# 22 of the 38 early expert tiles of a PEER layer in two float32r parts instead of whole float32 rows

## The chip, the cores and the metric

The kernel runs on one core of one Trainium2 chip. The metric is the time of one execution on the device in microseconds (us); of several runs the median is given. A profiled execution has a span, from its first to its last instruction, and a time of its own that is a little longer than the span.

The engines are named as in the profile: PE is TensorE (matmuls), PEld its weight loads, DVE is VectorE, ACT is ScalarE, POOL is GpSimd, SP is SyncE, which issues most of the DMAs.

## What is computed

An encoder block: a mixer (RWKV-7 and pooling), then an expert layer, then a last norm. The change is in the expert layer. Its reference, cut to what matters:

```python
def peer_ffn(h, wq, keys, u_tab, v_tab):
    def block_fn(xb):                       # 128 tokens at a time, 4 blocks
        q = (xb @ wq).reshape(T, PEER_HEADS, 2, PEER_KHALF)
        s = jnp.einsum('thpc,hpnc->thpn', q, keys)
        v1, i1 = lax.top_k(s[:, :, 0], 16)
        v2, i2 = lax.top_k(s[:, :, 1], 16)
        ...
        idx = jnp.take_along_axis(cidx, pos, axis=-1)
        gate = jax.nn.softmax(sc, axis=-1)
        ug = jnp.take(u_tab, idx, axis=0)
        act = jax.nn.gelu(jnp.einsum('td,thkd->thk', xb, ug))
        vg = jnp.take(v_tab, idx, axis=0)
        return jnp.einsum('thk,thkd->td', gate * act, vg)
```

There are 512 tokens, 1024 model dimensions, 16384 experts and 8 heads of 16 picks.

## The kernel before

The expert layer (`peer`, from line 948) treats three of the four token blocks, 384 tokens, densely and the fourth by gathering. For the dense blocks the 16384 experts are 128 tiles of 128. An **up tile** is the product of one tile of `u` with the 384 tokens, over 8 slices of the 1024 dimensions, followed by a Gelu on ACT into a tile `gl`. A **down step** multiplies `gl` by the gates `gt` of that tile of experts, and multiplies the result by the tile of `v` into six PSUM banks `o`.

Up tiles exist in two forms. `up_parts` (L990) takes a tile in two float32r parts: `split` (L978) casts the raw tile `ur` to `uh` on ACT (L980) and subtracts on DVE to get the low part `ul` (L982); then there are three matmuls for each of 8 slices, `uh` with `hh` (L994), `uh` with `hl` (L995) and `ul` with `hh` (L996), 24 in all. The generator `ups` (L1013) takes **early** tiles, which are computed before the down side starts, with whole float32 rows: one matmul for each slice, `ur` with `hx` (L1020), 8 in all. The profile shows each of these float32 matmuls as two records, so 16 a tile. There are 38 early tiles (608 records): ten whose `gl` is stored in DRAM for later, and 28 that stay in SBUF. The other 90 tiles go through `up` (L1003) inside the loop over down steps.

While `ups` runs, the rest of the selection runs beside it. For each token block DVE makes the top-16 picks (`top16`, `topk`: L1412 to L1471), and `transposed` (L1485) turns a dense block's picks and gates with three PE transposes (`sc<-ident`, L1491), a copy on ACT to `pk` (L1494) and a remainder on DVE (L1496). Then `encode` (L1172) makes for each 8 tokens a **code block** of three tiles on DVE, `a2` (L1187), `b1` (L1189) and `bh` (L1191); `b1` is then scaled by a remainder on DVE or POOL (L1194) or with eight small instructions on ACT (L1197). At most three code blocks are held (`NB = 3`). `gates` (L1201) multiplies a code block on PE in two halves of 8 matmuls (`pg`, L1212 and L1213), ACT copies each half to `sg` (L1215), and every second block SP writes `sg` to the DRAM tensor `gdram` (L1218). The down side reads it back as `gt`.

The order of all this is written as a string of letters, `PROG2`, one letter for one step of a generator (`u` is a step of `ups`, two slices of a tile; `e` and `p` are steps of `encode` and `gates`). A scheduler then places the instructions of each engine; on each engine they run in the placed order. PSUM has two buffers for `d` (up tiles) and two for `pg`; SBUF has three for `ur`, two for `uh` and two for `ul`.

Of the kernel before, what the change touches and what calls it, by code (L numbers as in the profile page):

```python
# [10 lines left out]
F32 = mybir.dt.float32  # L11
# [4 lines left out]
AF = mybir.ActivationFunctionType  # L16
# [7 lines left out]
DT = D // 128  # L24
# [38 lines left out]
SX = "VVVV"  # L63
SH = "VGVGVGVG"
NHF = 3
NST = 2
PORD = [6, 2, 7, 10, 3, 17, 19, 14, 11, 18]
PROG = 'mmmmsmmmmss2ms22sss2sms2msms2sssmssmm2smssmsmsmsmss2sms3smsmssmss2vvmp3msmmj32mj33mjm33jmggmm33mmjjmmv2m33SvSSSSvSSmSwSmSpSpSSgCSaaSSaaSSDalhSSSlfffffafhaSafSSaSfSaSSfaSSahaSSffflffhSahfaafafaaJJaafffJfhlfaaJafJaJabbfnbbfbbflnbbfbfbfbnfbbbbfbnbbbbnfbnnfbnoxoobxoxxoxoboxoooxboobxyyoooooyyXyXXXyXyXXXXyYYYYYYYYY'
# [79 lines left out]
def mixer(ctx, rs, tc, t, x_dram, x2_dram, ident, vec, vecs, dbg, load_vectors):  # L148
# [51 lines left out]
    with ExitStack() as s1:  # L200
        ld = s1.enter_context(tc.tile_pool(name="ld", bufs=1, side="right"))
        st = s1.enter_context(tc.tile_pool(name="st", bufs=NST, side="right"))
        x = [ld.tile([128, D], F32, name=f"x{i}") for i in range(NT)]
# [8 lines left out]
        for i in range(NT):  # L212
# [5 lines left out]
            for q in range(2):  # L218
                pt = bank([128, 4, 128])
                for d in range(4):  # L220
                    PE.transpose(pt[:, d], x[i][:, (4 * q + d) * 128:(4 * q + d + 1) * 128], ident)
                hf = st.tile([128, 4, 128], F32, name="hf", bufs=NHF)
                V.tensor_tensor(hf, pt, vecs("n1")[:, 4 * q:4 * q + 4, None].to_broadcast([128, 4, 128]), op=ALU.mult)
# [724 lines left out]
def peer(ctx, rs, tc, t, X2, x2_dram, ident, out, dbg):  # L948
    nc = tc.nc
    V, A, G, PE, SY = nc.vector, nc.scalar, nc.gpsimd, nc.tensor, nc.sync  # L950
    pool = lambda n, b, **k: ctx.enter_context(tc.tile_pool(name=n, bufs=b, **k))
    GT, DTS = 3, [1, 2, 0]
    ND = 128 * len(DTS)
# [5 lines left out]
    ps_d = pool("psd", 2, space=PSUM)  # L959
# [16 lines left out]
    E = {"V": V, "G": G}  # L976

    def split(src, n, pool, eng=V):  # L978
        hi = pool.tile([128, D], F32R, name=n + "h")
        A.copy(hi, src)  # L980
        lo = pool.tile([128, D], F32R, name=n + "l")
        eng.tensor_tensor(lo, src, hi, op=ALU.subtract)  # L982
        return hi, lo

    def up_load(e):
        raw = ub.tile([128, D], F32, name="ur", bufs=3)
        SY.dma_start(raw, t["uT"][e])
        return raw

    def up_parts(uh, ul):  # L990
        ps = ps_d.tile([128, ND], F32, name="d")
        for d in range(DT):
            c = slice(d * 128, d * 128 + 128)
            PE.matmul(ps, uh[:, c], hh[:, d, 0:ND], start=d == 0, stop=False)  # L994
            PE.matmul(ps, uh[:, c], hl[:, d, 0:ND], start=False, stop=False)  # L995
            PE.matmul(ps, ul[:, c], hh[:, d, 0:ND], start=False, stop=d == DT - 1)  # L996
            if d in (1, 3, 5):
                yield
        g = glp.tile([128, ND], F32, name="gl")
        A.activation(g, ps, AF.Gelu)  # L1000
        yield g
# [9 lines left out]
    early = later + list(range(AHEAD))  # L1011

    def ups():  # L1013

        raw = {e: up_load(e) for e in early[:3]}
        for k, e in enumerate(early):
            ur = raw.pop(e)
            ps = ps_d.tile([128, ND], F32, name="d")
            for d in range(DT):
                PE.matmul(ps, ur[:, d * 128:d * 128 + 128], hx[:, d], start=d == 0, stop=d == DT - 1)  # L1020
                if d in (1, 3, 5):
                    yield
            if k + 3 < len(early):
                raw[early[k + 3]] = up_load(early[k + 3])
            g = glp.tile([128, ND], F32, name="gl")
            A.activation(g, ps, AF.Gelu)  # L1026
            if e in later:
                SY.dma_start(gld[later.index(e)], g)
            else:
                Gl[e] = g  # L1030
            yield

    with ExitStack() as pa:
# [9 lines left out]
        hx = pa.enter_context(tc.tile_pool(name="hx", bufs=1)).tile([128, DT, ND], F32, name="hx")  # L1043
# [196 lines left out]
        def chained(gens):  # L1240
# [3 lines left out]
        ub = glp = None  # L1244
        order = ORDER
        streams = {z: stream(z, g, *needs) for z, g, *needs in (
            ("n", normed()), ("O", opened(), "n"), ("q", queries(), "n"), ("k", scores(), "n"), ("t", tops()),
            ("r", chained([choose(n, 0) for n in order])), ("R", chained([select(n) for n in order])),
            ("c", swap(), "kt"), ("e", encode(), "c"), ("p", gates(), "c"), ("u", ups(), "O"))}
        left = {"n": 12, "O": 1, "k": 16, "t": 64, "c": 1}  # L1250
        engines = [{"PE": PE, "V": V, "A": A, "G": G, "SY": SY}[z].engine for z in ORD.split(",")]
# [39 lines left out]
    with ExitStack() as pb:  # L1291
# [51 lines left out]
        for e in range(NE):  # L1343
            n = e + AHEAD
# [6 lines left out]
            raw = vb.tile([128, D], F32, name="vr")  # L1351
# [9 lines left out]
            for k in range(share(e), share(e + 1)):  # L1361
                u = vb.tile([128, D], F32, name="gat", bufs=6)
# [180 lines left out]
```

## Time and profile before

| | us |
|---|---|
| time, median of 3 runs | 1752.48 (1751.49 to 1756.0) |
| the profiled execution: its own time | 1755.74 |
| the profiled execution: its span | 1754.0 |
| PE busy in the span | 1633.1 (93%) |
| DVE busy | 1287.5 (73%) |
| ACT busy | 642.7 (37%) |
| POOL busy | 518.1 (30%) |
| up tiles with whole rows, L1020 | 215.8 busy, 608 records |
| up tiles in two parts, L994, L995, L996 | 242.3, 242.0, 242.2 busy, 720 records each |

Shares over the whole span hide that the stages differ. The early tiles run from 565.5 to 836.8 us of the span, the tiles in two parts from 836.8 us. A matmul's record reaches from its start to its modelled end, and records of neighbours overlap; the pace of a row of matmuls is therefore read from start to start.

### The profile page before, as it was taken

Reading aid. Unit: us, or ns where it says so; the run is one execution under the profiler, and the core shown is the slowest. Engines: PE = TensorE matmul, PEld = TensorE weight load, DVE = VectorE, ACT = ScalarE, POOL = GpSimd, SP = SyncE. Lnnn points to the kernel's source line nnn. Section 1 sums busy time; section 2 is a strip of 40 time slices with the busy share of each in tenths; the row PEclk is TensorE's granted clock in tenths of the full one; section 3 lists DMA queues with packets and bytes.
Section 4 is the critical chain, followed back from the end, with each engine's and each line's share of the span. In section 5 each row is a group of like instructions: output and inputs, shape, how many; then the busy total and the mean of one; then the engine's idle time right before and its main releaser. Section 6 shows DMA issues by size and latency. Waiting matters only on the chain.

```text
span 1754.0 us, 25849 instructions
## 1 busy us (share of the span) xinstructions
PE 1633.1 (93%) x9513; PEld 1317.4 (75%) x9513; DVE 1287.5 (73%) x2730; ACT 642.7 (37%) x1090; POOL 518.1 (30%) x355
## 2 busy tenths in 40 slices
PE   6888776899799799999999999999999999999997
PEld 5766664564587456566889999898989989898886
DVE  5665976446589999853467787777777887787776
ACT  4343331121433267353433333333333333333334
POOL 2331432000113000000104454444554554554430
PEclk8788887999899899999999999999999999999999
DMA  3354478760321365454989889989989998887774
GB/s 139 104 139 115 135 156 272 199 213 26 140 85 65 104 229 214 151 201 180 326 270 324 304 325 341 323 312 327 339 305 337 332 314 329 314 321 254 259 261 160
DMA packets 220191, 405.29 MB, mean 231 GB/s; under 512 B 38352, under 2 KB 137168, under 8 KB 216992
## 3 DMA queue, kind: packets, MB, share of 16 engines
q1 hardware_dynamic: 179680, 258.06, 45.1%
q0 software_dynamic: 39808, 144.52, 22.7%
q8 instruction: 75, 1.23, 0.3%
q10 hardware_dynamic: 576, 1.05, 0.2%
q14 instruction: 52, 0.43, 0.1%
HBM read 350.23 MB, written 53.35 MB: 230 GB/s over the span
## 4 chain that ended last, share of the span: by engine, by line
PE 73%; DVE 17%; DMA 5%; ACT 2%; issue 2%; SPq 1%; POOL 0%; DVEq 0%; ACTq 0%; POOLq 0%
PE o L1385 29%; PE d L996 7%; PE d L995 7%; PE d L994 7%; PE d L1020 6%; PE mm L815 2%; DMA UV<-vd 2%; PE a L500 2%; PE mm L323 2%; PE mm L321 1%; PE mm L322 1%; DMA gt<-gdram 1%; DVE pr L1467 1%; PE mm L1095 1%; DVE a L1187 1%
## 5 line engine op out<-in xcount | busy, mean ns | idle before, releaser
L1302 POOL DMA_INDIRECT gat<-in_peer_u,num x128 | 190.5, 1489 | 293.8 <-DVE gat L1308 243.5
L1302 POOL DMA_INDIRECT gat<-in_peer_v,num x128 | 198.4, 1550 | 214.0 <-DVE acc L1310 190.0
L996 PE MATMUL d<-hh,ul 128*128 128x384 f32 x720 | 242.3, 337 | 0.0
L994 PE MATMUL d<-hh,uh 128*128 128x384 f32 x720 | 242.2, 336 | 0.0
L995 PE MATMUL d<-hl,uh 128*128 128x384 f32 x720 | 242.0, 336 | 0.0
L1385 PE MATMUL o<-vl,wh 128*128 128x512 f32 x768 | 238.6, 392 | 2.3 <-DVE vl L982 2.3
L1385 PE MATMUL o<-vh,wh 128*128 128x512 f32 x768 | 238.4, 392 | 0.8 <-ACT wh L1369 0.8
L1385 PE MATMUL o<-vh,wl 128*128 128x512 f32 x768 | 238.3, 391 | 0.0
L1020 PE MATMUL d<-hx,ur 128*128 128x384 f32 x608 | 215.8, 499 | 8.0 <-ACT gl L1026 8.0
L980 ACT CAST uh<-ur 128x1024 fp32r<-128x1024 f32 x90 | 94.8, 1053 | 241.8 <-PE d L995 232.2
L1369 ACT CAST wh<-gl 128x384 fp32r<-128x384 f32 x128 | 65.7, 514 | 303.9 <-PE o L1385 296.0
L1371 DVE TENSOR_TENSOR wl<-gl,wh 128x384 fp32r<-128x384 f32 x128 | 71.3, 557 | 141.0 <-ACT wh L1369 140.2
L1385 PEld LDWEIGHTS o<-vl,wh 128*128 128x128 f32 x768 | 144.3, 188 | 34.9 <-DVE vl L982 3.4
L1385 PEld LDWEIGHTS o<-vh,wl 128*128 128x128 f32 x768 | 144.6, 188 | 31.2
L1020 PEld LDWEIGHTS d<-hx,ur 128*128 128x128 f32 x608 | 111.7, 193 | 72.0 <-ACT gl L1026 8.6
L1310 DVE SCALAR_TENSOR_TENSOR acc<-gat,wg,acc 128x1024 f32<-128x1024 f32 x128 | 163.8, 1280 | 0.9
L982 DVE TENSOR_TENSOR vl<-vr,vh 128x1024 fp32r<-128x1024 f32 x128 | 156.1, 1220 | 9.3 <-ACT vh L980 8.6
L1385 PEld LDWEIGHTS o<-vh,wh 128*128 128x128 f32 x768 | 143.4, 188 | 25.1 <-ACT wh L1369 1.1
L1308 DVE SCALAR_TENSOR_TENSOR gat<-gat,h2g 128x1024 f32<-128x1024 f32 x128 | 153.5, 1218 | 0.0
L980 ACT CAST vh<-vr 128x1024 fp32r<-128x1024 f32 x128 | 135.1, 1055 | 24.5 <-DMA vr<-in_peer_v 22.6
L982 DVE TENSOR_TENSOR ul<-ur,uh 128x1024 fp32r<-128x1024 f32 x90 | 109.9, 1222 | 44.1 <-ACT uh L980 44.0
L995 PEld LDWEIGHTS d<-hl,uh 128*128 128x128 f32 x720 | 135.3, 188 | 4.2
(364 smaller groups left out, 2741.8 us busy)
## 6 DMA issues: line engine op xcount, KB each, us to landing
ur<-in_uT SPq DMA_DIRECT2D x128, 512.0 KB, 5.3
vr<-in_peer_v SPq DMA_DIRECT2D x128, 512.0 KB, 4.1
gdram<-sg SPq DMA_DIRECT2D x24, 1024.0 KB, 3.9
gt<-gdram SPq DMA_DIRECT2D x16, 1536.0 KB, 14.3
wqk<-in_wqk SPq DMA_DIRECT2D x16, 576.0 KB, 3.5
gad<-gs SPq DMA_DIRECT2D x16, 512.0 KB, 3.3
GA<-gad SPq DMA_DIRECT2D x16, 512.0 KB, 4.8
w<-in_w_in SPq DMA_DIRECT2D x15, 512.0 KB, 6.7
```

Of the source, the lines that this page charges most:

```text
L980: A.copy(hi, src)
L982: eng.tensor_tensor(lo, src, hi, op=ALU.subtract)
L994: PE.matmul(ps, uh[:, c], hh[:, d, 0:ND], start=d == 0, stop=False)
L995: PE.matmul(ps, uh[:, c], hl[:, d, 0:ND], start=False, stop=False)
L996: PE.matmul(ps, ul[:, c], hh[:, d, 0:ND], start=False, stop=d == DT - 1)
L1020: PE.matmul(ps, ur[:, d * 128:d * 128 + 128], hx[:, d], start=d == 0, stop=d == DT - 1)
L1302: G.indirect_dma_start(out=u, out_offset=None, in_=t["peer_u" if k < NP else "peer_v"], in_offset=bass.IndirectOffsetOnAxis(ap=num[:, kk:k ...
L1308: V.scalar_tensor_tensor(u, u, 1.0, h2g, op0=ALU.mult, op1=ALU.mult, accum_out=dot[:, kk:kk + 1])
L1310: V.scalar_tensor_tensor(acc, u, wg[:, kk:kk + 1], acc, op0=ALU.mult, op1=ALU.add)
L1369: A.copy(wh, w)
L1371: wi = V.tensor_tensor(wl, w, wh, op=ALU.subtract)
L1385: PE.matmul(O[j][q], a[:, c], b[:, q * 512:(q + 1) * 512], start=e == 0 and n == 0, stop=e == NE - 1 and n == 2)
```

## The change

The first 16 early tiles (`UF = 16`) keep the whole float32 rows. The other 22 go through `split` and `up_parts`, as the 90 later tiles do, with the low part made on the engine that a string `UE` names for each tile, which is DVE (`V`) for all. The split of a tile is written after the second slice of the tile before it. The strings `PROG2` and `BLE` and the buffers are unchanged.

```diff
+UF = 16
+UE = 'VVVV...'
...
         raw = {e: up_load(e) for e in early[:3]}
+        parts = {}
         for k, e in enumerate(early):
-            ur = raw.pop(e)
-            ps = ps_d.tile([128, ND], F32, name="d")
-            for d in range(DT):
-                PE.matmul(ps, ur[:, d * 128:d * 128 + 128], hx[:, d], start=d == 0, stop=d == DT - 1)
-                if d in (1, 3, 5):
-                    yield
+            ur = raw.pop(e) if k < UF else None
+            if ur is not None:
+                ps = ps_d.tile([128, ND], F32, name="d")
+                for d in range(DT):
+                    PE.matmul(ps, ur[:, d * 128:d * 128 + 128], hx[:, d], start=d == 0, stop=d == DT - 1)
+                    if d == 1 and k + 1 >= UF and k + 1 < len(early):
+                        parts[k + 1] = split(raw.pop(early[k + 1]), "u", ub, E[UE[k + 1]])
+                    if d in (1, 3, 5):
+                        yield
+                g = glp.tile([128, ND], F32, name="gl")
+                A.activation(g, ps, AF.Gelu)
+            else:
+                for n, g in enumerate(up_parts(*parts.pop(k))):
+                    if n == 0 and k + 1 < len(early):
+                        parts[k + 1] = split(raw.pop(early[k + 1]), "u", ub, E[UE[k + 1]])
+                    if n < 3:
+                        yield
             if k + 3 < len(early):
                 raw[early[k + 3]] = up_load(early[k + 3])
-            g = glp.tile([128, ND], F32, name="gl")
-            A.activation(g, ps, AF.Gelu)
```

After the change the lines of `peer` from L978 on stand two lines lower and those behind `ups` thirteen lower.

Three places of the new order follow. In names such as `a_6424` the number tells code blocks apart.

**DVE, around the third low part.** Before, these rows run in the last third of the second dense block's encoding; `e_3768` collects the third dense block's picks.

```order
L1470 TENSOR_TENSOR pr<-pr 128x2x64
L1187 TENSOR_TENSOR a_6433<-ior,pk_5828 128x1024
L1189 TENSOR_TENSOR b_6435<-ior,pk_5828 128x1024
L1471 TENSOR_REDUCE e_3768<-pr 128x2x16
L1191 TENSOR_TENSOR bh<-b_6435,pk_5828 128x1024
```

Now, at the place where the third dense block's picks are collected:

```order
L1480 TENSOR_TENSOR pr<-oh,f_6603 128x512 x2
L1200 TENSOR_TENSOR a_6540<-ior,pk_5828 128x1024
L1202 TENSOR_TENSOR b_6542<-ior,pk_5828 128x1024
L984 TENSOR_TENSOR ul<-ur,uh 128x1024
L1204 TENSOR_TENSOR bh<-b_6542,pk_5828 128x1024
L1482 TENSOR_TENSOR pr<-pr 128x2x128
L984 TENSOR_TENSOR ul<-ur,uh 128x1024
L1207 TENSOR_TENSOR b_6542<-b_6542,pk_5828 128x1024
```

The third and the fourth low part stand between the rows of one code block; they are two of nine that stand ahead of the remainder `pk` of the third dense block (L1509, L1496 of before).

**ACT, before the third cast.** Before, the Gelu of an early tile follows the exponential of `gate`:

```order
L1197 ACTIVATE b_6390<-b_6390,lo_5896 128x128 x6
L1477 ACT_TABLE_LOAD
L1477 ACTIVATE gate<-gate 128x128
L1215 ACTIVATE sg<-pg 128x128x4 x2
L1026 ACT_TABLE_LOAD
L1026 ACTIVATE gl<-d 128x384
L1215 ACTIVATE sg<-pg 128x128x4 x2
```

Now the casts stand among them:

```order
L1210 ACTIVATE b_6426<-b_6426,lo_5896 128x128 x6
L1490 ACT_TABLE_LOAD
L1490 ACTIVATE gate<-gate 128x128
L1228 ACTIVATE sg<-pg 128x128x4 x2
L1002 ACT_TABLE_LOAD
L1002 ACTIVATE gl<-d 128x384
L982 CAST uh<-ur 128x1024
L1228 ACTIVATE sg<-pg 128x128x4 x2
L982 CAST uh<-ur 128x1024
```

The third and fourth cast of an early tile stand behind the same two table loads.

**PE, at the transposes of the third dense block.** Before:

```order
L1213 MATMUL pg<-b_6608,a_6606 128x128
L1020 MATMUL d<-hx,ur 128x384 x21
L1491 MATMUL sc<-ident,e_3768 128x128 x2
L1491 MATMUL sc<-ident,gate 128x128
L1020 MATMUL d<-hx,ur 128x384 x12
L1212 LDWEIGHTS a_6741
```

Now (the first three rows end a run of 66 matmuls, where one of 21 stood):

```order
L996 MATMUL d<-hh,uh 128x384
L997 MATMUL d<-hl,uh 128x384
L998 MATMUL d<-hh,ul 128x384
L1504 MATMUL sc<-ident,e_3768 128x128 x2
L1504 MATMUL sc<-ident,gate 128x128
L996 MATMUL d<-hh,uh 128x384
```

The code blocks and transposes keep their places among the slices of the early tiles; each slice of a tile is now three matmuls.

## Rows read from the trace of the kernel before

**Rows 1.** The page: busy tenths of PE and DVE, granted clock, in 40 slices.

```profile
PE   6888776899799799999999999999999999999997
DVE  5665976446589999853467787777777887787776
PEclk8788887999899899999999999999999999999999
```

**Rows 2.** Busy time in three stretches: length, then PE, PEld, DVE, ACT, POOL (instructions), granted clock, DMA.

```profile
691.95:731.40 39.45, 36.23 (x216) 23.68 (x214) 39.42 (x188) 19.05 (x40) 0.00 (x0) 0.98 0.47 166
731.40:836.80 105.40, 105.40 (x535) 66.47 (x534) 45.50 (x85) 46.32 (x110) 1.89 (x1) 0.99 0.54 190
900.00:1700.00 800.00, 799.64 (x3977) 718.20 (x3977) 617.89 (x774) 285.62 (x387) 377.90 (x248) 1.00 0.88 310
```

**Rows 3.** The chain that ended last, 729 to 747 us: start, length, what.

```profile
729.52 0.20 DVE gateg L1476
729.75 0.31 ACT gateg L1477
730.06 0.49 ACT sg L1215
...
731.60 14.54 PE d L1020 x42
746.14 0.33 PE sc L1491 x3
```

**Rows 4.** Timeline of PE, whole-row tiles and code blocks: start, length, what [idle before].

```profile
691.95 0.22 PE L1212 MATMUL pg<-bh,a 128*128 128x128 f16 x1
...
692.87 0.86 PE L1020 MATMUL d<-hx,ur 128*128 128x384 f32 x2
...
715.64 9.24 PE L1020 MATMUL d<-hx,ur 128*128 128x384 f32 x28
724.72 0.22 PE L1212 MATMUL pg<-bh,a 128*128 128x128 f16 x1
...
730.59 0.26 PE L1212 MATMUL pg<-bh,a 128*128 128x128 f16 x1 [2.80 <-ACT sg L1215]
...
731.40 14.74 PE L1020 MATMUL d<-hx,ur 128*128 128x384 f32 x42
745.98 0.38 PE L1491 MATMUL sc<-ident,e 128*128 128x128 f32 x2
```

**Rows 5.** Timeline of PE, tiles in two parts, 54 matmuls of which three stand here.

```profile
836.80 0.63 PE L994 MATMUL d<-hh,uh 128*128 128x384 f32 x1
...
837.45 0.33 PE L996 MATMUL d<-hh,ul 128*128 128x384 f32 x1
...
846.30 0.34 PE L996 MATMUL d<-hh,ul 128*128 128x384 f32 x1
```

**Rows 6.** The page, groups of the split: count, busy us, mean ns, idle before.

```profile
L980 ACT CAST uh<-ur 128x1024 fp32r<-128x1024 f32 x90 | 94.8, 1053 | 241.8 <-PE d L995 232.2
L982 DVE TENSOR_TENSOR ul<-ur,uh 128x1024 fp32r<-128x1024 f32 x90 | 109.9, 1222 | 44.1 <-ACT uh L980 44.0
```

**Rows 7.** Timeline of DVE, 686 to 854 us.

```profile
686.58 0.67 DVE L1187 TENSOR_TENSOR a<-ior,pk 128x1024 f16<-128x1024 f16 x1
...
689.39 0.68 DVE L1187 TENSOR_TENSOR a<-ior,pk 128x1024 f16<-128x1024 f16 x1
690.00 0.69 DVE L1189 TENSOR_TENSOR b<-ior,pk 128x1024 f16<-128x1024 f16 x1
...
738.31 0.28 DVE L1482 TENSOR_TENSOR gateg<-gateg,gs 128x128 f32<-128x128 f32 x1
747.02 0.29 DVE L1496 TENSOR_TENSOR pk<-sc,pk 128x128 f16<-128x128 f32 x1 [8.43 <-ACT pk L1494]
...
852.38 1.22 DVE L982 TENSOR_TENSOR ul<-ur,uh 128x1024 fp32r<-128x1024 f32 x1
853.52 1.22 DVE L982 TENSOR_TENSOR vl<-vr,vh 128x1024 fp32r<-128x1024 f32 x1
```

**Rows 8.** Timeline of ACT: a table load, and eight scalings of one code block.

```profile
702.77 1.28 ACT L1477 ACT_TABLE_LOAD   x1
...
749.89 2.48 ACT L1197 ACTIVATE b<-b,lo 128x128 f16<-128x128 f16 x8 [0.30 <-DVE bh L1191]
```

More of the change, by code (lines that the diff above doesn't have):

```diff
@@ L65 @@
 NHF = 3
+UF = 16
+UE = 'VVVVVVVVVVVVVVVVVVVVVVVVVVVVVVVVVVVVVVVVVVVVVVVVVVVVVVVVVVVVVVVVVVVVVVVVVVVVVVVV'
 NST = 2
```

## The prediction

> **What bounds the kernel now.** I read the 40 slices first [rows 1]: from the twenty-second on PE is at 9 and DVE at 7 or 8, so the down side is PE's; ahead of it the two lines change places, DVE at 9 where PE is at 7 and then PE at 9 where DVE is at 6 and 5. The change lies in that change of places, so I cut the stretch of the 22 tiles out with a table of windows [rows 2]. From 691.95 to 731.40 us DVE is busy for 39.42 of 39.45 us; from 731.40 to 836.80 us PE is busy for all of 105.40 us and DVE for 45.50. The chain that ended last agrees [rows 3]: it runs along DVE up to `gateg` at 729.52, crosses ACT (an exponential and a copy of `sg`) and then stays on PE, 14.54 us of whole-row matmuls first. So a saving on PE counts at its full size after 731 us, and what is added to DVE before that may count too. From 900 to 1700 us PE is busy 799.64 of 800 us, with the same instructions after the change: whatever is won before the down side is kept.
>
> **What an early tile costs on PE.** From 715.64 to 724.72 us 28 records of whole-row matmuls start, one in 0.3243 us [rows 4]; a tile has 16, so 5.19 us. In two parts, 51 matmuls lie between the starts at 837.45 and 846.30 us, 0.1735 us each [rows 5]; a tile has 24, so 4.16 us. The difference is 1.03 us a tile and 22.6 us for 22. Both paces are of the full clock and of the same shapes that the change uses (384 tokens, 128 by 128 weights).
>
> The Trainium skill ("FP8 and Floating Point Precision", section "TensorE Precision Notes") says that true FP32 takes four passes through the array. Three passes for four would save a quarter of 5.19 us, an estimate of 1.30 us a tile and 28.5 us in all. The trace shows less, since a part takes 0.1735 us where a quarter of a whole row takes 0.162; I go by the trace.
>
> **The sum over the stretch.** PE has from 691.95 to 836.80 us, 144.85 us, 360 records of whole rows (22.5 tiles, 116.7 us), 24 code blocks at 0.92 us (one runs from 691.95 to 692.87 [rows 4], 22.1 us) and 0.33 us of transposes [rows 3]: 139.2 us. The other 5.7 us are losses: one wait of 2.80 us for `sg` at 730.59 [rows 4], after which the 42 records take 14.58 us where the pace gives 13.62, at a granted clock that the table puts at 0.98 and 0.99 over the stretches; the rest is small. After the change four whole-row matmuls are left (2.6 us) and 528 matmuls of parts come in (91.6 us): 116.6 us of work, 22.6 us less. What decides is how the 5.7 us of losses change.
>
> **What is added elsewhere.** ACT gets 22 casts of 1.053 us (23.2 us), DVE 22 subtractions of 1.222 us [rows 6], which follow each other at 1.14 us [rows 7]: 25.1 us. DVE has 60 us free in the second stretch [rows 2] and nothing in the first, so place matters. I add the paces of DVE's rows in the new order, from the first row that it shares with the old one (the `a` step at 686.58). Code passes go at 0.6 us [rows 7], the selection rows at what they take in the trace; the same addition over the old order lands on `gateg` within 0.2 us of 738.31 [rows 7].
>
> *To the third low part:* 20 code passes (12.0 us), three low parts (3.4) and the selection rows between them (7.8) are 23.2 us, so it is ready at 709.8 us. PE comes there with 73 code-block matmuls (4.2 us), four whole rows (2.6) and 50 of parts (8.7) after 691.95, at about 707.6. It waits for 2 us. The third cast doesn't make it later: behind the two table loads (1.28 us each [rows 8]) it ends at about 707.3.
>
> *To the third dense block:* 26 code passes, nine low parts (10.3 us) and 26.8 us of selection put `pk` at 739.3 us. PE has its transposes done at 733.5 plus the 2 us, so at 735.5 to 736. Before, it was DVE that waited for PE here, 8.43 us [rows 7]. From `pk` on the first code block takes 2.7 us on DVE and 2.48 us of scalings on ACT [rows 8], to 744.5. PE covers this with the 36 matmuls that stand between (6.2 us), to 742.3: a wait of 2.2 us.
>
> *The rest:* from there PE has 68.8 us of work. DVE has 58 us, with the last 13 low parts. ACT had 46.32 us in 105.40 [rows 2] and gets 13 casts (13.7): 60 us. Neither is full, but both run in order and are at five sixths of PE's time. No row shows waits of this kind; from below they cost nothing, from above one pair of cast and subtraction uncovered at each third tile (13/3 x 2.27 = 10 us). I take 3 us, near the lower end, since the splits are written a tile ahead and before the change PE had no idle time in this stretch [rows 2].
>
> So the stretch ends at 744.5 + 68.8 + 3 = 816.3 us instead of 836.8: 20.5 us earlier. The long wait at 730.59 goes, because the exponential of `gateg` moves behind the third block's first codes; waits of 2.0, 2.2 and 3 us come. The DMAs stay as many: a `ur` tile is loaded once in either form, and its buffer comes free earlier, when the low part is made. SP's queue carries the same loads and writes, and what starts the down side (54 matmuls, then `gt` from DRAM) has the same distance from the last code block. The profiled execution took 1755.74 us, 3.3 above the median; 20.5 us less is 1735.2 beside it and 1732 beside the median.
>
> **Rivals.** *The new waits hide.* If the low parts are ready in time and the 5.7 us go as well, the gain is 22.6 + 5.7 = 28 us: 1724. Against it stands that DVE is full to 731 us [rows 2] and nine low parts are put there.
>
> *DVE stays the bound.* Its chain up to `pk` gets nine low parts and is not shortened by PE's gain. Should the code blocks behind them come late as well, the 10.3 us are lost once and the gain is 12 us: 1740. The Trainium skill ("TensorE: Matmul & The Clock Gate", "Architectural detail: the array is 16x 32x32, not 1x 128x128") says that ACT and DVE take their queues strictly in order. The trace agrees in the 2.80 us that PE waited for a copy standing behind an exponential.
>
> *The queues interlock, and the kernel is slower.* A low part waits for its cast, the cast for scalings and table loads ahead of it, and the codes behind the low part wait with it; PE stands. Its place is the second stretch, where codes and splits alternate. Uncovered, a tile costs a cast and a subtraction, 2.27 us [rows 6]; 22 tiles cost 50 us, and less the 22.6 the result is 27 us slower: 1780. It decides from the point where more than 1.03 us is lost for each tile. For it speaks that two `uh` and two `ul` leave one tile of lead; against it that DVE and ACT have a sixth of the stretch free.
>
> *It evens out.* The same mechanism at half that price takes the 22.6 us: 1750 to 1755. In all of them the clock could add: the one wait of 2.80 us had a loss of about 1 us behind it.
>
> **How the numbers follow.** The forecast, 1727 to 1738, has 0.62; hidden waits (1722 to 1727) 0.10; DVE as bound (1738 to 1747) 0.16; evened out 0.06; slower 0.06. The range from 1724 to 1744 leaves out the last two, the upper end of the third and the lower end of the second, some 2 in 10. A measurement of this kernel can tell about 0.3%, 5.3 us, from no change: faster 0.88, within 0.06, slower 0.06.
>
> **What would show it.** In the profile after, the whole-row records fall to 256, the parts rise to 112 tiles (896 of each line) at a pace of 0.1735 us; the last matmul ahead of the first down step, at 846.30 before, comes about 20 us earlier; PE's long idle time ahead of a `d` matmul is for `ul` near 710 us and for `ACT b` near 743 us, 2 us each, and no wait of 2.8 us for `sg` is left. DVE is full until about 739 us and above 80% from there to the down side. It is wrong if the pace of the parts beside the selection is not 0.1735, if PE's waits in the stretch sum to over 12 us, or if the down side starts earlier but ends no earlier, for instance because `gt` or `vr` land late.

## The result and the profile after

The change takes 1734.28 us (median of 4 runs, 1731.09 to 1735.49), the kernel before 1754.24 us (median of 4, 1751.49 to 1760.95). The ratio is 0.9878, 95% interval 0.9845 to 0.991: 20 us less by the medians and 21 by the ratio, which is one of means, where 20.5 were forecast (1732, range 1724 to 1744). The profiled execution has an own time of 1731.09 us and a span of 1729.4, against 1755.74 and 1754.0.

Of the 24.6 us between the two spans, 3.3 are not the change's: the first matmul of the early tiles starts at 562.44 us where it stood at 565.7, with the same instructions ahead of it. From there to the first matmul of the down side the stretch is 261.6 us (562.44 to 824.03) instead of 281.8 (565.7 to 847.46), 20.2 us shorter; the rest, about 1 us, is the down side. The length of this stretch, called **the stretch** below, is the measure of all the experiments. It has one weakness: every kernel is scheduled anew, and matmuls of later tiles can move across its end. Before the change 54 matmuls in two parts stand between the last early tile and the first matmul of the down side, after it 57, so 0.5 us of the stretch after is work brought forward. Each stretch comes from one profiled execution; the change's own, taken twice, is 261.6 and 262.1.

The 40 slices of the page after, as [rows 1]:

```profile
PE   6888876899899799999999999999999999999997
DVE  5665986437589999995667777777778878787776
PEclk8788887999899899999999999999999999999999
```

From the fifteenth to the eighteenth slice (605 to 778 us) PE and DVE are both at 9. Before, DVE left that level two slices earlier and fell to 3 and 4; it now falls to 5 and 6 only. The windows after, as [rows 2] (length, then PE, PEld, DVE, ACT, POOL, granted clock, DMA), with one more over the whole stretch, first from the trace of before and then from that of after:

```profile
565.00:847.00 282.00, 263.40 (x1451) 170.90 (x1449) 215.39 (x776) 138.56 (x327) 7.14 (x3) 0.98 0.52 181
562.00:824.00 262.00, 242.58 (x1629) 194.22 (x1627) 240.91 (x799) 158.95 (x350) 7.59 (x3) 0.97 0.56 199
691.95:731.40 39.45, 38.59 (x287) 36.29 (x287) 39.45 (x141) 23.81 (x46) 0.00 (x0) 1.00 0.59 208
731.40:816.50 85.10, 83.45 (x638) 78.90 (x637) 69.26 (x151) 58.98 (x124) 2.33 (x1) 1.00 0.62 218
900.00:1700.00 800.00, 800.00 (x3963) 716.38 (x3962) 623.78 (x777) 286.62 (x387) 378.87 (x250) 1.00 0.88 312
```

Read the whole stretch first. PE's busy time fell from 263.40 us to 242.58, and DVE's rose from 215.39 to 240.91. The two are now level, each busy for 92 to 93% of the stretch. From 731.40 to 816.50 us DVE is at 81%, as forecast, and the granted clock is 1.00 where it was 0.98 and 0.99. The down side is PE's as before: 800 of 800 us.

The groups of the split after, as [rows 6] (count, busy us, mean ns, idle before):

```profile
L998 PE MATMUL d<-hh,ul 128*128 128x384 f32 x896 | 301.9, 337 | 0.8 <-DVE ul L984 0.8
...
L982 ACT CAST uh<-ur 128x1024 fp32r<-128x1024 f32 x112 | 117.8, 1052 | 259.9 <-PE d L997 254.6
...
L984 DVE TENSOR_TENSOR ul<-ur,uh 128x1024 fp32r<-128x1024 f32 x112 | 136.7, 1220 | 40.4 <-ACT uh L982 36.4
```

All 112 tiles are in parts, at the prices of before. Over the whole kernel PE lost only 0.8 us to the low part of an up tile that was late.

### Where PE waits now

Timeline of PE after (start, length, what, [idle before <- releaser]), as [rows 4]; the first row is the code block that starts at 691.95 in the trace of before:

```profile
688.84 0.22 PE L1225 MATMUL pg<-bh,a 128*128 128x128 f16 x1
...
692.02 0.22 PE L1225 MATMUL pg<-bh,a 128*128 128x128 f16 x1 [1.41 <-ACT sg L1228]
...
696.46 0.22 PE L1226 MATMUL pg<-b,a 128*128 128x128 f16 x1
696.48 0.42 PE L996 MATMUL d<-hh,uh 128*128 128x384 f32 x1
696.74 0.34 PE L997 MATMUL d<-hl,uh 128*128 128x384 f32 x1
696.92 0.34 PE L998 MATMUL d<-hh,ul 128*128 128x384 f32 x1
...
707.24 0.44 PE L998 MATMUL d<-hh,ul 128*128 128x384 f32 x1 [0.79 <-DVE ul L984]
...
746.38 0.22 PE L1225 MATMUL pg<-bh,a 128*128 128x128 f16 x1 [1.49 <-ACT sg L1228]
...
822.64 0.34 PE L998 MATMUL d<-hh,ul 128*128 128x384 f32 x1
...
824.03 0.73 PE L1398 MATMUL o<-vh,wh 128*128 128x512 f32 x2 [0.54 <-ACT wh L1382]
```

The shared code block stands 3.11 us earlier in this execution (688.84 for 691.95); add that to a time of after to compare it with one of before. From this block to the first down step it is 135.2 us, 155.5 before. Three waits of over half a microsecond are left ahead of the down side, 3.7 us in all, and the 2.80 us for `sg` [rows 4] is not among them.

The first and the last of these are for `sg`, whose copy stands in ACT's queue behind something that itself waits. Timeline of ACT after, at both:

```profile
689.56 1.04 ACT L982 CAST uh<-ur 128x1024 fp32r<-128x1024 f32 x1 [2.35 <-DMA ur<-in_uT]
690.51 1.02 ACT L1210 ACTIVATE b<-b,lo 128x128 f16<-128x128 f16 x3
691.40 1.05 ACT L1228 ACTIVATE sg<-pg 128x512 f32<-128x512 f32 x2
...
745.45 0.44 ACT L1210 ACTIVATE b<-b,lo 128x128 f16<-128x128 f16 x1 [1.63 <-DVE bh L1204]
745.76 1.06 ACT L1228 ACTIVATE sg<-pg 128x512 f32<-128x512 f32 x2
```

At 689.56 the second cast of an early tile waited 2.35 us for the load of its tile (the first, at 682.40, did not wait), and the scalings and the copy of `sg` waited behind it, though their own data were there. A split made ahead of its tile wants its load earlier too, and it is ACT's whole queue that pays, not only the tile. At 745.45 a scaling waited for DVE, and `sg` behind it.

### The profile page after: what moved, and what is told of

It is laid out like the page before. It is cut to its first block, busy times and chain, and to the rows that moved or that the text cites. A ratio compares the mean times of both kernels' runs of the same rounds, so it can differ in the third digit from the quotient of the medians.

```text
span 1729.4 us, 26282 instructions
## 1 busy us (share of the span) xinstructions
PE 1610.6 (93%) x9689; PEld 1338.9 (77%) x9689; DVE 1312.7 (76%) x2752; ACT 661.8 (38%) x1112; POOL 517.6 (30%) x355
## 4 chain that ended last, share of the span: by engine, by line
PE 68%; DVE 19%; DMA 4%; ACT 2%; issue 2%; SPq 1%; POOL 0%; DVEq 0%; ACTq 0%; POOLq 0%
PE o L1398 30%; PE d L996 8%; PE d L998 8%; PE d L997 8%; PE mm L817 3%; DMA UV<-vd 2%; DMA gt<-gdram 2%; DVE bh L1204 1%; DVE a L1200 1%; DVE b L1202 1%; PE mm L325 1%; PE mm L323 1%; PE a L502 1%; PE mm L1108 1%; PE mm L324 1%
## 5 line engine op out<-in xcount | busy, mean ns | idle before, releaser
L996 PE MATMUL d<-hh,uh 128*128 128x384 f32 x896 | 303.9, 339 | 0.0
L998 PE MATMUL d<-hh,ul 128*128 128x384 f32 x896 | 301.9, 337 | 0.8 <-DVE ul L984 0.8
L997 PE MATMUL d<-hl,uh 128*128 128x384 f32 x896 | 301.3, 336 | 0.0
L982 ACT CAST uh<-ur 128x1024 fp32r<-128x1024 f32 x112 | 117.8, 1052 | 259.9 <-PE d L997 254.6
L997 PEld LDWEIGHTS d<-hl,uh 128*128 128x128 f32 x896 | 168.5, 188 | 4.2
L996 PEld LDWEIGHTS d<-hh,uh 128*128 128x128 f32 x896 | 168.4, 188 | 3.7
L998 PEld LDWEIGHTS d<-hh,ul 128*128 128x128 f32 x896 | 168.4, 188 | 0.9 <-DVE ul L984 0.9
L984 DVE TENSOR_TENSOR ul<-ur,uh 128x1024 fp32r<-128x1024 f32 x112 | 136.7, 1220 | 40.4 <-ACT uh L982 36.4
```

## The experiments

One caution holds for all of them: an edit also changes the order in which the scheduler places other rows, so no experiment changes one thing alone. Where it is seen to matter, it is said.

### Does PE's pace carry the gain? Half the tiles, then more of them

Whole rows for the first 27 tiles, so that 11 go in parts:

```diff
-UF = 16
+UF = 27
```

> UF = 27: only the last 11 early tiles go in two parts. Measure: the stretch from the first matmul of an early tile to the first matmul of the down side, 281.8 us before and 261.6 us with the change. Theory (each tile gives its 1.03 us on PE, less what the alternation costs): 11 tiles give 11.3 us on PE, the wait of 2.80 us for sg stays, so the stretch is 271 to 274 us and the time 0.5% below before. Rival (the gain came from the moved exponential and the wait and clock loss that went with it, not from the tiles): the stretch is 279 to 283 us, the time as before.

Measured: 1746.4 us against 1752.74, ratio 0.9956 (0.994 to 0.9971); the stretch is 271.4 us, 10.4 shorter than before. Eleven tiles at 1.03 us are 11.3 us. PE's 2.79 us for `sg` is still there, at 725.75 us. So the gain comes with the number of tiles, at the price of the pace, and not from that wait.

Then 12, 20 and 8 tiles in whole rows (26, 18 and 30 in parts), each the same one-line edit:

```diff
-UF = 16
+UF = 12
...
+UF = 20
...
+UF = 8
```

> UF = 12: 26 early tiles in two parts. Measure: the stretch from the first early matmul to the first down-step matmul, 261.6 us with the change (UF = 16) and 265.6 us with UF = 8. Theory (ahead of the third dense block's pk DVE is full, so four more low parts of 1.14 us, 4.6 us, go on its path, and PE's 4.1 us come off a path with little wait): the stretch is 260 to 265 us, no measurable difference from the change. Rival (PE's saving counts): 257 to 259 us.

> UF = 20: 18 early tiles in two parts; the four tiles that go back to whole rows lie between 694 and 716 us. Theory (PE's 4.1 us return, DVE's 4.6 us come off, and the two are nearly level ahead of pk): 261 to 265 us. Rival (each tile gives its 1.03 us on PE wherever it lies): 265 to 267 us. Rival (DVE sets the end): 256 to 259 us.

> UF = 8: 30 early tiles in two parts, eight more, all in the stretch in which DVE is full. Theory (DVE sets the end there, so PE's further 8.2 us are paid back by eight more low parts of 1.14 us, 9.1 us): the stretch is 259 to 264 us, the time within 0.3% of the change. Rival (PE's saving counts wherever the tiles lie): 30 tiles give 30.9 us less alternation, the stretch is 252 to 256 us and the time 0.4% to 0.5% below the change.

The change itself ran again beside the kernels with 12 and 20:

> The change itself beside the two others: the stretch 261 to 262 us, the time 1.0% to 1.3% below before.

| whole-row tiles | in parts | us | before, run beside it | ratio (95%) | stretch |
|---|---|---|---|---|---|
| 27 | 11 | 1746.4 | 1752.74 | 0.9956 (0.994 to 0.9971) | 271.4 |
| 20 | 18 | 1741.28 | 1753.81 | 0.9936 (0.9918 to 0.9953) | 270.5 |
| 16, again | 22 | 1735.2 | 1753.81 | 0.9896 (0.9878 to 0.9914) | 262.1 |
| 12 | 26 | 1734.34 | 1753.81 | 0.9891 (0.9872 to 0.9911) | 262.1 |
| 8 | 30 | 1734.54 | 1752.74 | 0.9901 (0.9875 to 0.9926) | 265.6 |

Below 16 whole-row tiles the gain stops: no setting is faster than the change by more than the intervals tell. With 12 the forecast range was met; with 8 the stretch is 1.6 us over it. Why the gain stops is in the windows of the kernel with 8 (columns as above):

```profile
640.00:690.00 50.00, 43.87 (x333) 37.30 (x332) 46.91 (x148) 36.55 (x85) 0.00 (x0) 0.97 0.54 186
690.00:740.00 50.00, 48.81 (x367) 46.33 (x365) 50.00 (x177) 33.41 (x65) 0.00 (x0) 1.00 0.58 208
```

and in its PE timeline:

```profile
636.41 0.27 PE L1226 MATMUL pg<-b,a 128*128 128x128 f16 x1 [3.78 <-POOL b L1207]
...
673.35 0.22 PE L1225 MATMUL pg<-bh,a 128*128 128x128 f16 x1 [4.17 <-ACT sg L1228]
```

DVE is full or nearly so, and PE stands for codes and for `sg`, while its own work got eight tiles shorter. With 12 the four tiles win 4.1 us on paper, and the stretch stays. PE's waits alone don't say why: those for `ul` are 5.0 us (the longest 2.52) instead of 0.8, but those for `sg` are 0.5 instead of 4.8. The granted clock adds to them: it is 0.89 from 645 to 660 us and 0.83 from 730 to 740 in that kernel, where the change has 1.00, which is some 3.3 us at half the clock each time and up to 3.3 us of PE's time in all, an estimate.

With 20 all that was expected missed. Four tiles should have given back 4.1 us (265.7); it is 270.5. Two waits stand out, 4.9 us together. PE's timeline in that kernel:

```profile
735.53 0.44 PE L996 MATMUL d<-hh,uh 128*128 128x384 f32 x1 [2.75 <-ACT uh L982]
735.81 0.34 PE L997 MATMUL d<-hl,uh 128*128 128x384 f32 x1
735.99 0.27 PE L1504 MATMUL sc<-ident,e 128*128 128x128 f32 x1
736.10 0.27 PE L1504 MATMUL sc<-ident,gate 128*128 128x128 f32 x1
738.50 0.69 PE L998 MATMUL d<-hh,ul 128*128 128x384 f32 x1 [2.13 <-DVE ul L984]
```

and ACT's:

```profile
732.43 0.31 ACT L1490 ACTIVATE gateg<-gateg 128x128 f32<-128x128 f32 x1 [3.36 <-DVE gateg L1489]
732.76 1.28 ACT L1002 ACT_TABLE_LOAD   x1
734.05 0.49 ACT L1002 ACTIVATE gl<-d 128x384 f32<-128x384 f32 x1
734.44 1.99 ACT L982 CAST uh<-ur 128x1024 fp32r<-128x1024 f32 x2
```

Here two casts stand behind the exponential of `gateg`, which waits for DVE, and behind a table load. DVE is busy for 19.90 of the 20 us to 740, so the low part that follows is late as well. Behind the two waits the granted clock is at its lower level:

```profile
737.00:743.00 6.00, 4.50 (x14) 4.50 (x15) 6.00 (x12) 0.19 (x1) 0.00 (x0) 0.50 0.48 156
```

From 738.99 to 743 us PE works at half the clock, which costs it some 2 us, an estimate. That the 4.9 us of the two waits match the missing 4.8 is chance: the lower clock comes on top, and the waits of 1.41, 0.79 and 1.49 us of the change are not there. The order differs too, since in the change the exponential of `gateg` comes only at 758.14 us. So the place of the splits and of that exponential in ACT's queue can cost as much as four tiles give. The forecast interlock exists, then, as single waits at such places.

### What does the low part cost, twice and without PE's gain?

The low part of each early tile made twice on DVE, the second time for nothing:

```diff
...
         eng.tensor_tensor(lo, src, hi, op=ALU.subtract)
+        if twice:
+            eng.tensor_tensor(lo, src, hi, op=ALU.subtract)
...
-                        parts[k + 1] = split(raw.pop(early[k + 1]), "u", ub, E[UE[k + 1]])
+                        parts[k + 1] = split(raw.pop(early[k + 1]), "u", ub, E[UE[k + 1]], True)
...
```

> The change with each early tile's low part made twice on DVE (the second writes the same values), 22 x 1.14 = 25 us more of DVE. Theory (DVE sets the pace up to the third dense block's pk and is at five sixths after it): nine more low parts put pk 10 us later, 13 more fill DVE to over PE's 69 us behind it; the stretch is 271 to 277 us, 10 to 15 us longer than with the change. Rival (DVE is off the path, its free time covers all): the stretch is 261 to 264 us.

Measured: 1743.3 us against 1752.74, ratio 0.9948 (0.9929 to 0.9968); the stretch is 276.0 us, 14.4 longer than with the change. Not all of that is cost: the stretch holds 619 matmuls of parts where the change's holds 585, so 34 matmuls of later tiles, 5.9 us at 0.1735, have moved across its end. That leaves 8.5 us, and the times agree: 0.9948 of before against 0.9896 for the change run again is 9.1 us. Twenty-two more subtractions at 1.14 us are 25.1 us on DVE; about a third of it shows. Over the stretch, in that kernel:

```profile
563.00:839.00 276.00, 253.94 (x1662) 202.06 (x1660) 266.18 (x819) 160.81 (x352) 8.10 (x3) 0.97 0.54 187
```

DVE is busy for 96% of it. So the change left some slack on DVE, but not 25 us. The range of 271 to 277 us was met by luck: `pk`, which was to come 10 us later, comes 172.6 us into the stretch, against 174.3 in the change. Seventeen subtractions stand ahead of it instead of nine, but DVE has 628 instructions up to there instead of 676, so other rows were moved behind `pk`, and the added time shows there: 103.4 us from `pk` to the down side instead of 87.3.

Then the splits with PE's work of before: whole rows for all 38 tiles, and 22 splits that nobody reads.

```diff
-            ur = raw.pop(e) if k < UF else None
-            if ur is not None:
+            ur = raw.pop(e)
+            if True:
...
-                        parts[k + 1] = split(raw.pop(early[k + 1]), "u", ub, E[UE[k + 1]])
+                        split(raw[early[k + 1]], "u", ub, E[UE[k + 1]])
```

> The matmuls of before (whole float32 rows for all 38 early tiles), but the 22 tiles are also split as in the change, and the parts are not used: the added work of DVE and ACT alone. Theory (what lies on the full DVE ahead of 731 us costs, what lies behind it is free): the stretch is 285 to 293 us, 3 to 11 us longer than before. Rival (PE covers the splits wherever they lie): 281 to 284 us. Rival (the queues interlock): over 295 us.

Measured: 1756.33 us against 1752.74, ratio 1.0013 (1.0001 to 1.0025); the stretch is 282.5 us, 0.7 more than before. The rival was right: 25 us of subtractions and 23 us of casts cost nearly nothing in sum, although DVE had been full to 731 us [rows 2]. That is a net figure. The wait of 2.80 us for `sg` [rows 4] is gone in this kernel, by the order in ACT's queue, and smaller waits have come, 0.94 us for a Gelu at 742.65 and 1.11 us for the first code block behind `pk`. Without the one that went, the splits would have cost some 3.5 us, an estimate (0.7 and 2.8). DVE's timeline and its windows in that kernel:

```profile
750.66 0.29 DVE L1509 TENSOR_TENSOR pk<-sc,pk 128x128 f16<-128x128 f32 x1
```

```profile
691.95:740.00 48.05, 47.65 (x253) 30.27 (x252) 47.95 (x194) 26.68 (x51) 0.00 (x0) 1.00 0.58 198
740.00:848.00 108.00, 105.66 (x549) 68.89 (x548) 68.41 (x118) 62.76 (x128) 1.89 (x1) 0.98 0.55 183
```

Both engines are full to 740 us, and `pk` comes at 750.66 where it stood at 747.02 [rows 7] (2.4 of the 3.6 us because the whole stretch starts later here, at 568.1). So a full DVE was hardly a bound: PE had as much to do, and before, the 8.43 us that DVE waited ahead of `pk` [rows 7] were slack, which took up most of the 10.3 us of nine low parts. With PE's work taken away DVE's load shows more, 9 us of 25. Together the two runs speak for the balance of the two engines, and not the busy share of one, as what decides; a doubled low part on PE's work of before, which would settle it, was not run.

### PE's third part away

No low part of the early tiles and no matmul with it; the product with the low part is left out of the result:

```diff
+        if not low:
+            return hi, None
...
-            PE.matmul(ps, uh[:, c], hl[:, d, 0:ND], start=False, stop=False)
-            PE.matmul(ps, ul[:, c], hh[:, d, 0:ND], start=False, stop=d == DT - 1)
+            PE.matmul(ps, uh[:, c], hl[:, d, 0:ND], start=False, stop=ul is None and d == DT - 1)
+            if ul is not None:
+                PE.matmul(ps, ul[:, c], hh[:, d, 0:ND], start=False, stop=d == DT - 1)
...
```

> The change without the low parts of the early tiles: no subtraction, and two matmuls for a slice instead of three (the product of the low part with the tokens is left out of the result). PE loses 176 x 0.1735 = 30.5 us, DVE 25 us. Theory (after the change PE sets the pace, DVE's selection follows close behind): DVE's list puts pk at about 729 us, PE has some 51 us left from the first code block of the third dense block, so the stretch is 233 to 241 us. Rival (PE alone): 261.6 - 30.5 = 231 us or less. Rival (DVE sets it, at the end of its list): over 245 us.

Measured: 1709.61 us against 1753.25, ratio 0.9755 (0.9726 to 0.9784); the stretch is 240.1 us, 21.5 shorter than the change's and within the range. Here too the order differs: 77 matmuls of later tiles stand ahead of the down side instead of 57, 3.5 us of work brought forward. So the gain is 25.0 us, and the times agree: 0.9755 of before against 0.9896 is 24.7 us. PE has 176 matmuls fewer, 30.5 us at 0.1735, and DVE 25 us less. Of the 5.5 us that are missing, PE has a wait of 2.0 us for a code and waits of 1.5 for `uh`, and its granted clock from 690 to 735 us is 0.96 where the change has 1.00; they were not taken apart further. Less work on both engines still doesn't give PE's share in full.

### The low part on POOL

POOL is all but idle in this stretch [rows 2], so the low parts were moved there: of the first nine tiles in parts, of all 22, and, with 8 whole-row tiles, of the first 17. The edit for nine, the others likewise:

```diff
-UE = 'VVVVVVVVVVVVVVVVVVVVVVVVVVVVVVVVVVVVVV...'
+UE = 'VVVVVVVVVVVVVVVVGGGGGGGGGVVVVVVVVVVVVV...'
```

> The change with the first nine of the 22 low parts, those ahead of the third dense block's pk, made on POOL, which has one instruction in that stretch (a subtraction of this shape takes it 2.4 us in the queries of the kernel before). Measure: the stretch from the first early matmul to the first down-step matmul, 281.8 us before, 261.6 us with the change. Theory (the nine low parts on DVE are what PE waits for near 707 and 746 us, and little more): 10.3 us less on DVE brings PE at most these waits of 0.8 and 1.5 us, the stretch is 258 to 262 us and the time within 0.3% of the change. Rival (DVE's chain sets the end, by all of its 10 us): the stretch is 250 to 254 us.

> The change with all 22 low parts on POOL. Theory (behind pk PE is the bound, so DVE's lighter load gives nothing there, and a low part of 2.4 us still fits into a tile's 4.2 us): the stretch is 258 to 263 us. Rival (POOL is late with a cast and 2.4 us for each tile and its scaling of a code block stands behind them): 265 to 275 us.

> UF = 8 with the low parts of the tiles 8 to 24 on POOL and of the others on DVE. Theory (with eight more tiles in parts PE is ahead and DVE's own selection sets the pace, and in the run with UF = 8 the eight low parts on DVE added to it): with the 17 low parts off DVE the stretch is 253 to 259 us, 7 to 12 us shorter than with UF = 8 on DVE (265.6 us). Rival (it is PE's order and its waits for code blocks, not DVE's work, that hold UF = 8 back): 263 to 267 us as with DVE.

All three missed, all on the slow side. Nine: 1748.73 us against 1753.25, ratio 0.9985 (0.9967 to 1.0002), stretch 279.3. All 22: 1755.22, ratio 1.001 (0.9996 to 1.0024), stretch 282.2. With 8 whole-row tiles: 1767.19, ratio 1.0077 (1.0048 to 1.0106), stretch 294.7. With nine, most of the change's gain is gone (2.4 us of 20.2 are left in the stretch); with more, all of it. The timeline of the kernel with nine, POOL and DVE at the third and fourth low part:

```profile
706.71 5.19 POOL L984 TENSOR_TENSOR ul<-ur,uh 128x1024 fp32r<-128x1024 f32 x2 [15.05 <-ACT uh L982]
```

```profile
705.54 0.68 DVE L1200 TENSOR_TENSOR a<-ior,pk 128x1024 f16<-128x1024 f16 x1
...
707.05 2.61 DVE L1204 TENSOR_TENSOR bh<-b,pk 128x1024 f16<-128x1024 f16 x1
709.58 2.48 DVE L1482 TENSOR_TENSOR pr<-pr 128x256 f16<-128x256 f16 x1
711.98 0.68 DVE L1207 TENSOR_TENSOR b<-b,pk 128x1024 f16<-128x1024 f16 x1
```

While POOL runs its two subtractions, DVE completes two instructions, 2.61 and 2.48 us long, and as soon as POOL is done a code pass takes 0.68 us again. The groups of these two lines and of POOL's low parts from 690 to 740 us (count, busy us, mean ns, idle before):

```profile
L1204 DVE TENSOR_TENSOR bh<-b,pk 128x1024 f16<-128x1024 f16 x5 | 5.3, 1066 | 0.0
...
L1482 DVE TENSOR_TENSOR pr<-pr 128x256 f16<-128x256 f16 x8 | 4.3, 555 | 0.0
...
L984 POOL TENSOR_TENSOR ul<-ur,uh 128x1024 fp32r<-128x1024 f32 x7 | 17.9, 2570 | 39.8 <-ACT uh L982 39.8
```

and in the change:

```profile
L1204 DVE TENSOR_TENSOR bh<-b,pk 128x1024 f16<-128x1024 f16 x6 | 4.1, 679 | 0.0
...
L1482 DVE TENSOR_TENSOR pr<-pr 128x256 f16<-128x256 f16 x8 | 2.1, 284 | 0.0
```

So a low part on POOL takes about 2 us of DVE's time (2.61 less 0.68, 2.48 less 0.28), more than the 1.14 us that it takes on DVE itself. Over these 50 us seven groups of DVE instructions got longer, by 13 us in all for seven low parts.

That is some 7 us for nine low parts (nine times 1.9 less 1.14, an estimate), and the stretch lost 17.7. The order took part in the rest. ACT's timeline in that kernel:

```profile
737.83 0.31 ACT L1490 ACTIVATE gateg<-gateg 128x128 f32<-128x128 f32 x1 [10.06 <-DVE gateg L1489]
738.04 1.03 ACT L982 CAST uh<-ur 128x1024 fp32r<-128x1024 f32 x1
739.09 1.28 ACT L1002 ACT_TABLE_LOAD   x1
740.38 0.49 ACT L1002 ACTIVATE gl<-d 128x384 f32<-128x384 f32 x1
```

and in the change:

```profile
758.14 0.31 ACT L1490 ACTIVATE gateg<-gateg 128x128 f32<-128x128 f32 x1
```

The exponential of `gateg` stands in ACT's queue ahead of the third dense block's codes here, and behind the first of them in the change. It waits 10.06 us for DVE, the Gelu stands behind it, and PE waits 7.49 us for the Gelu (at 740.93); with all 22 low parts on POOL that wait is 7.5 us too. Besides, PE waits 3.86 us for `sg` at 691.23, behind a cast that waited 4.23 us for its load, and the granted clock is 0.91 from 690 to 740 us, where the change has 1.00. How much of the loss is DVE's time and how much is the order was not separated, and the kernel with 17 low parts on POOL was not taken apart.

The Trainium skill ("SBUF — State Buffer", section "Who interferes with whom") says that a VectorE instruction with two inputs in SBUF contends with a GpSimd instruction that reads SBUF, and that the ports which they share are locked for one of the two at a time. The 2.61 and 2.48 us beside POOL's 2.57 agree with that.

## Why the prediction was right

**PE's pace (22.6 us): right.** 256 whole-row records and 896 of each part are left, the parts at 0.1735 us beside the selection too (696.74 to 696.92). Eleven tiles gave 10.4 us, twenty-two 20.2, so up to 22 the saving is each tile's own; the 11.3 us of eighteen are less for the reasons told above. The 28.5 us that the forecast set aside would have been 14.2 for eleven tiles, and neither is near.

**The losses: the sum held, the terms did not.** The forecast put 7.8 us of losses (816.3 less 691.95 less 116.6) in place of 5.7. Of the matmuls in two parts ahead of the down side the 54th, the last one before the change, moved by 20.55 us (822.64 and 3.11 against 846.30), so they are 7.7. They consist of other things, so it is luck that the sum agrees this well:

- *The wait for the third low part,* 2 us forecast, is 0.79. The low part is ready at 707.2 us, 710.3 on the clock of before, where 709.8 was forecast: DVE's sum over its rows was right within 0.5 us. PE came later than forecast (706.45, that is 709.6 instead of 707.6), because it had lost 1.41 us at 692.02 and some at each change between codes and parts.
- *The 1.41 us at 692.02* was not foreseen. "The DMAs stay as many" is true but leaves out that a split needs its load earlier.
- *The third dense block.* `pk` at 736.72 us, 739.8 on the clock of before, against 739.3; right. But PE starts the block's matmuls at 739.96 with no wait, since each runs as its own scaling is done, and the forecast had made it wait for the last of eight. The wait comes in the second half of the second code block, 1.49 us at 746.38, through `sg`.
- *The 3 us of small waits* are mostly no waits: the first part behind a code block takes 0.26 us to the next start (696.48 to 696.74) where 0.1735 is the pace. At some 32 changes this is 2.8 us. Before the change a whole-row record behind a code block took 0.374 us to the next start instead of 0.3243, 1.7 us in all, so part of the 5.7 us was of this kind. About 1.2 us of the losses remain without a name.

**The wait of 2.80 us goes:** yes, and not because of PE's gain. With the unused splits, where no tile is in parts, it is gone too: there the copies of `sg` (the last at 730.09) stand ahead of the exponential's table load at 731.94 in ACT's queue, where before a copy stood behind the exponential [rows 3]. With 11 tiles in parts it stays, 2.79 us.

**"What is added to DVE before 731 may count too": hardly by itself.** The unused splits cost 0.7 us, or some 3.5 without the wait that went with them. DVE's load counts more once PE has less to do. The rival "DVE stays the bound" was wrong at 22 tiles and fits 30, where DVE is busy for all of 690 to 740 us; with 26 the lower clock takes part too.

**The down side** begins 20.2 us earlier and keeps it; its first waits are 0.54 and 0.58 us, so `gt` and `vr` are not late for PE.

## What to carry to other kernels

Cost a saving at the engine that it relieves, per tile and by the pace of the same shape in the same kernel, and then add up, in the order of the new program, when the other engines deliver. Follow each moved instruction's own input too: one early wait for a load holds everything behind it in that queue. When two engines are level, stop moving work between them, and try an idle third engine only after looking at what the busy one does while it runs.

## What the runs showed of the hardware

- A subtraction of 128x1024 float32 on POOL (2.57 us in the mean) holds DVE up: it stretches DVE instructions with two inputs from 0.68 to 2.61 us and from 0.28 to 2.48.
- A float32r part that follows 16-bit matmuls of 128 columns takes 0.086 us more than the pace of 0.1735, so finer mixing of codes and parts costs PE time that no wait shows.
- With 20 whole-row tiles PE waits 2.75 us up to 735.53 and 2.13 us up to 738.50. The granted clock is 1.00 from 730 to 736.5 us, 0.50 from 737 to 743, the lower of the two levels (1.2 GHz), and 1.00 again from 744 to 760. At the lower level the parts start 0.32 us apart (738.99, 739.31, 739.63) instead of 0.1735. In the change, where PE is busy for all of 720 to 740 us, the granted clock is 1.00. A wait can therefore cost more than its length.
